# Links between the sublayers of a transformer and a recurrent block, handled four k-tiles at a time

## The chip, the cores and the metric

The kernel runs on one core of one Trainium2 chip, as one launch. The metric is the device time of that core in microseconds (us). A core has a matrix engine (TensorE, "PE" in the profile, its weight loads "PEld"), VectorE ("DVE"), ScalarE ("ACT"), GpSimd ("POOL") and SyncE ("SP"), which issues all DMAs of this kernel.

## The reference, cut to what matters

Two blocks run one after the other in fp32 on 512 tokens of width 1024. The first is two layers of a transformer with 256 further context tokens that share all weights. Each layer has three sublayers, an FFN, a mixing sublayer (two kinds of attention and a Fourier mix), and a second FFN. Between any two of them stands the same arithmetic, per token, with gate, scale and shift vectors per layer, sublayer and stream:

```
y  = rms_norm(sublayer output, g_post)            # end of a sublayer ("post")
x  = x + weight * gate * y
h  = rms_norm(x, g_pre) * (1 + scale) + shift     # start of the next ("pre")
# FFN:  (silu(h @ w1_gate) * (h @ w1_up)) @ w2,   width 2816
```

The second block (a gated recurrence with a state-space scan, then a stick-breaking attention layer) follows on 528 tokens and isn't touched.

## The kernel before, in words

**Layout.** All activations lie transposed: 128 features on the partitions, tokens on the free axis. The 1024 features are eight k-tiles. The residual stream is `X[0..7]`, one tile of 128x528 per k-tile, and `XC` for the context. A sublayer's input is `H[0..7]`, each 128 x 2 x 768, its rounded part "hi" and the remainder "lo"; columns 0 to 511 are latent tokens, 512 to 767 context. Every fp32 product is three matmuls (`mm3`: weight hi by hi, weight hi by lo, weight lo by hi). `Y[0..7]` (128x768 each) gathers a sublayer's output.

**Streams.** The work goes by streams of columns: `cx` (context, 256 wide), `lat` (latent, 512), and its halves `la` and `lb` (256 each). In a sublayer that starts with an FFN, the first of six groups of hidden tiles runs by `cx`, `la`, `lb`; later groups run by halves of all 768 columns with a seven-product scheme (`strassen`) and then `ffn2` over `cx` and `lat`.

**Links.** `link` (line 1240) chains `post` (line 499) and `pre` (line 515) for one stream. Both begin with `rstd`: a column sum of squares on TensorE (L463), a Newton square root on DVE (L474 to L482), a diagonal matrix on DVE (L484), and a matmul with ones (L489) that leaves 1/rms of each token, on all partitions, in PSUM as `r`. Then, for each k-tile, `post` does one DVE instruction for y times gate times r (L507), one DVE add into x (L509), one ACT square (L446, L449) and one add into the running sum (L450, on DVE or POOL by turns). `pre` does, for each k-tile, x times scale times r on DVE (L525), the shift and the rounding on ACT (L526: hi), and the remainder on DVE (L527: lo). So h comes k-tile by k-tile, and the first matmul of the next sublayer can start after the first one.

**Order.** TensorE's order is written by a planner, `run`: generators yield expected times, positive for TensorE time, negative for a wait, and the planner interleaves the one that matters ("crit") with work that fills in. The link of one stream is placed beside another stream's matmuls. The order fixed by these plans is kept on the chip. The other engines' queues and the DMA queue are ordered at build time by the framework's scheduler, and each runs in its order. A flag of the planner, `yfree`, is set by the end of a `post` (L512); in the first mixing sublayer the transposes of the attention values (`vt`, L950) wait for it in the plan, because their results lie in `Y`, and the two rope tables are loaded into `Y` after it.

**PSUM.** `pg` tiles (two buffers) take most products; `bank` tiles (four buffers) are used by `strassen`, by `rstd` in FFN sublayers, and for output tile 1 of `ffn2` (line 771 on). The evacuation of an `ffn2` product is an ACT copy (L786) in the first group and a DVE add into `Y` (L788) in the others.

**Spill.** During an FFN sublayer `X` and `XC` are moved to DRAM and their space holds `strassen`'s sums (`Halves`, line 212 on); they come back in the last group.

Of the kernel before, what the change touches and what calls it, by code (L numbers as in the profile page):

```python
# [211 lines left out]
class Halves:  # L212
# [3 lines left out]
    def __init__(self, b, pool, n):  # L216
        self.b, self.n = b, n
        q = lambda k0, t0: [tuple(b.H[k][:, j, t0 : t0 + n] for j in range(2)) for k in range(k0, k0 + 4)]
        self.B11, self.B12, self.B21, self.B22 = q(0, 0), q(0, n), q(4, 0), q(4, n)
        if n == XW // 2:  # L220
            own = [pool.tile([P, n], F32R, name=f"t{i}") for i in range(11)]
            xc = b.xc.tile([P, KD * NC], F32R, name="tc", tag="xc", bufs=1)
            own += [xc[:, i * n : (i + 1) * n] for i in range(5)]
            own += [b.perm.tile([P, T2], F32R, name=f"tx{k}", tag=f"x{k}", bufs=1)[:, :n] for k in range(KD)]
# [39 lines left out]
class Builder:  # L264
# [228 lines left out]
    def square_x(self, st):  # L493
# [2 lines left out]
            yield -1.8 * (0.2 + 0.9 * st.n / 512)  # L496
        yield -2

    def post(self, st, l, sub, nxt):

        nc = self.nc
        f = st.n / 512
        yield -0.455 * (2.6 + 1.6 * f)
        r = yield from self.rstd(st.s, st.n, D)
        for k in range(KD):
            u = self.ftile(st.n, "u")
            nc.vector.scalar_tensor_tensor(out=u, in0=st.y(k), scalar=self.modG[l][:, st.v, sub, k : k + 1], in1=r, op0=ALU.mult, op1=ALU.mult)  # L507
            x = st.x(k)
            nc.vector.tensor_tensor(out=x, in0=u, in1=x, op=ALU.add)  # L509
            self.add_sq(nxt, k, nxt.x(k), nc.gpsimd if k % 2 == 0 else None)  # L510
            yield -(0.4 + 1.5 * f)
        self.yfree = True  # L512
        yield -1.72 * (2.2 + 1.8 * f)

    def pre(self, st, l, sub):

        nc = self.nc
        r = yield from self.rstd(st.s, st.n, D)
        yield from self.wait_for((l, sub))
        for k in range(KD):  # L520
            u = self.ftile(st.n, "u")
            a = self.modA[l][:, st.v, sub, k : k + 1]
            b = self.modc[l][:, st.v, 24 * sub + k : 24 * sub + k + 1]
            hi, lo = st.h(k)
            nc.vector.scalar_tensor_tensor(out=u, in0=st.x(k), scalar=a, in1=r, op0=ALU.mult, op1=ALU.mult)  # L525
            nc.scalar.activation(hi, u, AF.Identity, bias=b)  # L526
            nc.vector.scalar_tensor_tensor(out=lo, in0=u, scalar=b, in1=hi.bitcast(F32), op0=ALU.add, op1=ALU.subtract)  # L527
            yield -0.85 * (0.1 + 1.2 * st.n / 512)

    def pre2(self, st, gain, d=D):  # L530

# [168 lines left out]
    def strassen(self, pool, l, wi, i0, mids, h):  # L700

        nc = self.nc
        n = h.n
        sub = lambda o, a, b: nc.vector.tensor_tensor(out=o, in0=a, in1=b, op=ALU.subtract)  # L704
        new = lambda nm: pool.tile([P, n], F32, name=nm, tag=nm, bufs=1)
        for ii, mid in enumerate(mids):
            A = self.wsums(self.I["wf1"][l, wi, i0 + ii])
            b1, b4, b2, b3 = (self.bank()[:, :n] for _ in range(4))

            def mm(i, p, b, start):  # L710
                yield from self.mm3(p, A[i], [(k, *x) for k, x in enumerate(b)], start=start, more=not start)
# [17 lines left out]
            sg = pool.tile([P, XW // 2], F32, name="sg", tag="sg", bufs=2)[:, :n]  # L729
# [12 lines left out]
    def ffn1(self, pool, l, wi, i0, mids, ss, ticks=False):  # L742
        nc = self.nc
        for ii, mid in enumerate(mids):
            wg, wu = self.early or self.wblock(self.I["wf1"][l, wi, i0 + ii], 2048, 2)
            self.early = None
            sgs = []
            for w in (wg, wu):
                for st in ss:
                    p = self.pg()[:, : st.n]  # L750
                    yield from self.mm3(p, w, st.rhs())
                    if w is wg:
                        sg = pool.tile([P, XW // 2], F32, name="sg", tag="sg", bufs=2)[:, : st.n]
                        nc.scalar.activation(sg, p, AF.Silu)
                        sgs.append(sg)
                    else:
                        m = self.ftile(st.n, "m")
                        nc.vector.tensor_tensor(out=m, in0=p, in1=sgs.pop(0), op=ALU.mult)  # L758
                        self.split(mid[:, 0, st.cs], mid[:, 1, st.cs], m)
            if ticks and ii % 2 == 0:  # L760
                yield from self.tick()

    def ffn2(self, l, wi, off, mids, ss, first, last, ticks, cb=None):
        nc = self.nc
        n = 2 * len(mids) * P
        for m2 in range(4):
# [3 lines left out]
            for mm in range(2):  # L770
# [6 lines left out]
                for i, st in enumerate(ss):  # L777
# [126 lines left out]
    def mix(self, l, streams, lasts, pend, exits):  # L904
# [4 lines left out]
        with ExitStack() as es:  # L909
# [31 lines left out]
            entry.first = True  # L941

            def vt(kind, i, base, t, offs):

# [240 lines left out]
            side = Task(side())  # L1185
            if full:

                cx.y = lambda k: src[k][:, cx.cs]
            self.run([attention()], [side])
            o_split(lat, (0, 1, 2))  # L1190
            if full:
                self.run(exits[:1], [o_proj(lat)])
                cx.y = lambda k: self.Y[k][:, cx.cs]
# [5 lines left out]
    def block1(self):  # L1199
        self.left, self.right = ExitStack(), ExitStack()  # L1200
        perm = self.perm = self.pool(self.ctx, "perm")
        xtile = lambda k: perm.tile([P, T2], F32, name=f"x{k}", tag=f"x{k}", bufs=1)
        self.X = [xtile(k) for k in range(KD)]
# [10 lines left out]
        AX_, AC_ = [away.tile([P, T2], F32, name=f"ax{k}") for k in range(KD)], away.tile([P, KD * NC], F32, name="ac")  # L1214

        def spill(out, first=False):

            if out and not first:
                self.dma(AC_, self.XC)
                for k in range(KD):  # L1220
                    self.dma(AX_[k], self.X[k])
            if not out:
                xctile()
                self.dma(self.XC, self.I["cin"].rearrange("p k n -> p (k n)") if first else AC_)
                for k in range(KD):
                    self.X[k] = xtile(k)
                    self.dma(self.X[k], self.I["xin"][:, k, :] if first else AX_[k])

        H = self.H = [hy.tile([P, 2, XW], F32R, name=f"h{k}") for k in range(KD)]
        self.Y = [hy.tile([P, XW], F32, name=f"y{k}") for k in range(KD)]  # L1230

        def stream(c0, n, v, xt, x0):
            st = Stream(c0, n, v, xt, x0, lambda k: (H[k][:, 0, c0 : c0 + n], H[k][:, 1, c0 : c0 + n]))
            st.y = lambda k: self.Y[k][:, c0 : c0 + n]
            return st

        lat, cx = stream(XL, NL, 0, self.X, META), stream(XC, NC, 1, XCt, 0)
# [669 lines left out]
```

## Time and profile before

| | |
|---|---|
| runs shown | 3799.95, 3806.11, 3950.75 us; median 3806.11 |
| the profiled execution's own time | 3801.48 us |
| its span (first to last instruction) | 3799.7 us |
| mean granted TensorE clock | 0.959 of full |
| TensorE matmul busy | 92% of the span |
| DVE, ACT, POOL busy | 62%, 45%, 37% |

The span is the time from the first instruction to the last; the execution's own time is 1.8 us longer. Idle time of an engine counts only where TensorE then waits. The granted clock has two levels, 1.0 (2.4 GHz) and 0.5 (1.2 GHz); at the lower one each matmul takes twice as long while it counts as busy.

### The profile page before, as it was taken

The page shows a single profiled execution, that of the slowest core. Times are in us where ns is not written, and L with a number is a line of the kernel's source. Part 1 is how long each engine was busy: PE and PEld are TensorE (multiplying, and loading weights), DVE is VectorE, ACT ScalarE, POOL GpSimd, SP SyncE. Part 2 cuts the span into 40 slices and gives each one's busy share as a digit, 9 for nine tenths or more (in the row PEclk, how much of TensorE's full clock was granted, in tenths as well). Part 3 has the DMA queues.
Part 4 walks back from the last instruction along what each step waited for, and adds up shares of the span by engine and source line. Part 5 has one row for each costly group of instructions (what it writes and reads, how often), then busy time and mean ns, then how long its engine had stood idle before and what let it go on. Part 6 is the DMA issues. An engine that isn't in the chain of part 4 may idle for free.

```text
span 3799.7 us, 61164 instructions
## 1 busy us (share of the span) xinstructions
PE 3504.7 (92%) x23260; PEld 3128.4 (82%) x23260; DVE 2364.0 (62%) x4769; ACT 1708.1 (45%) x3599; POOL 1400.0 (37%) x1151
## 2 busy tenths in 40 slices
PE   7899998998979999988999979888998898999997
PEld 5788897777878888888889967688887877999886
DVE  5844458667784444786445586667567776555546
ACT  5433334456543323454323445554444635635544
POOL 4533343211344333345333431145555433333112
PEclk8999998999989999999999989999999989999998
DMA  7433424212344343443342321242333311234112
GB/s 270 136 125 128 136 75 142 91 56 86 118 127 134 122 134 122 145 145 98 126 138 72 129 91 51 69 133 80 101 99 118 119 44 48 76 116 136 60 48 76
DMA packets 125437, 410.38 MB, mean 108 GB/s; under 512 B 14035, under 2 KB 25814, under 8 KB 123350
## 3 DMA queue, kind: packets, MB, share of 16 engines
q1 hardware_dynamic: 125142, 406.47, 33.5%
q8 instruction: 182, 2.98, 0.3%
q14 instruction: 113, 0.93, 0.1%
HBM read 397.90 MB, written 8.52 MB: 107 GB/s over the span
## 4 chain that ended last, share of the span: by engine, by line
PE 53%; DVE 15%; issue 5%; ACT 5%; POOL 2%; DMA 1%; ACTq 0%; DVEq 0%; POOLq 0%; SPq 0%
PE pg L421 9%; PE pg L422 9%; PE pg L423 9%; PE bank L416 7%; PE bank L421 4%; PE bank L423 3%; PE bank L422 3%; DVE op L353 2%; DVE ss L450 1%; PE po L611 1%; POOL op L353 1%; ACT op L347 1%; PE po L844 1%; PE psw L868 1%; PE po L1830 1%
## 5 line engine op out<-in xcount | busy, mean ns | idle before, releaser
L353 POOL TENSOR_TENSOR op<-raw,op 128x512 fp32r<-128x512 f32 (+1 forms) x660 | 891.2, 1351 | 1488.2 <-ACT op L347 1259.1
L347 ACT CAST op<-raw 128x512 fp32r<-128x512 f32 (+2 forms) x1178 | 709.9, 606 | 821.8 <-PE pg L423 421.3
L353 DVE TENSOR_TENSOR op<-raw,op 128x512 fp32r<-128x512 f32 (+2 forms) x518 | 402.6, 779 | 224.2 <-ACT op L347 217.7
L421 PE MATMUL pg<-h,op 128*128 128x256 f32 (+1 forms) x1440 | 480.1, 333 | 61.7 <-DVE m L758 26.5
L422 PE MATMUL pg<-h,op 128*128 128x256 f32 (+1 forms) x1440 | 467.9, 325 | 4.6 <-DVE h L527 3.3
L423 PE MATMUL pg<-h,op 128*128 128x256 f32 (+1 forms) x1440 | 462.3, 321 | 1.0 <-DVE op L353 0.6
L421 PE MATMUL pg<-mid,op 128*128 128x512 f32 (+1 forms) x1106 | 386.3, 349 | 13.6 <-ACT mid L347 5.3
L422 PE MATMUL pg<-mid,op 128*128 128x512 f32 (+1 forms) x1106 | 379.2, 343 | 1.8 <-DVE mid L353 1.7
L423 PE MATMUL pg<-mid,op 128*128 128x512 f32 (+1 forms) x1106 | 378.8, 342 | 0.0
L421 PEld LDWEIGHTS pg<-h,op 128*128 128x128 f32 x1440 | 293.6, 204 | 86.7 <-DVE m L758 29.2
L422 PEld LDWEIGHTS pg<-h,op 128*128 128x128 f32 x1440 | 292.7, 203 | 23.2 <-DVE h L527 11.1
L423 PEld LDWEIGHTS pg<-h,op 128*128 128x128 f32 x1440 | 293.1, 204 | 16.0 <-DVE op L353 1.0
L416 PE MATMUL bank<-h,op 128*128 128x384 f32 (+1 forms) x1704 | 293.5, 327 | 9.4 <-DVE u L704 9.4
L353 POOL TENSOR_TENSOR op<-ws,op 128x512 fp32r<-128x512 f32 x142 | 191.7, 1350 | 276.8 <-ACT op L347 276.8
L416 PEld LDWEIGHTS bank<-h,op 128*128 128x128 f32 x1704 | 280.9, 190 | 12.3 <-DVE u L704 12.3
L421 PEld LDWEIGHTS pg<-mid,op 128*128 128x128 f32 x1106 | 208.4, 188 | 75.0 <-DVE y L788 29.2
L788 DVE TENSOR_TENSOR y<-pg,y 128x256 f32<-128x256 f32 (+1 forms) x252 | 141.1, 562 | 198.2 <-PE pg L423 197.6
L422 PEld LDWEIGHTS pg<-mid,op 128*128 128x128 f32 x1106 | 208.6, 189 | 27.0 <-DVE mid L353 3.5
L423 PEld LDWEIGHTS pg<-mid,op 128*128 128x128 f32 x1106 | 208.3, 188 | 26.1
L421 PE MATMUL bank<-h,op 128*128 128x384 f32 (+1 forms) x636 | 206.4, 324 | 0.0
L423 PE MATMUL bank<-h,op 128*128 128x384 f32 (+1 forms) x636 | 203.6, 320 | 0.0
L422 PE MATMUL bank<-h,op 128*128 128x384 f32 (+1 forms) x636 | 203.6, 320 | 0.0
(434 smaller groups left out, 8430.1 us busy)
## 6 DMA issues: line engine op xcount, KB each, us to landing
raw<-wf SPq DMA_DIRECT2D x326, 512.0 KB, 3.7
mraw<-wmod SPq DMA_DIRECT2D x128, 512.0 KB, 4.7
raw<-win SPq DMA_DIRECT2D x58, 512.0 KB, 3.7
raw<-ewin SPq DMA_DIRECT2D x48, 512.0 KB, 3.6
raw<-owin SPq DMA_DIRECT2D x40, 512.0 KB, 3.6
raw<-wout SPq DMA_DIRECT2D x32, 512.0 KB, 3.6
raw<-wf SPq DMA_DIRECT2D x32, 384.0 KB, 3.2
raw<-ewout SPq DMA_DIRECT2D x24, 512.0 KB, 3.6
```

The source lines that it names most:

```text
L347: self.nc.scalar.copy(hi, src)
L353: eng.tensor_tensor(out=lo, in0=src, in1=hi.bitcast(F32), op=ALU.subtract)
L416: mm = self.nc.tensor.matmul if not more else lambda *a, **kw: self.nc.tensor.matmul(*a, skip_group_check=True, **kw)
L421: mm(p, lhsT=a, rhs=xh, start=start and i == 0, stop=False)
L422: mm(p, lhsT=a, rhs=xl, start=False, stop=False)
L423: mm(p, lhsT=b, rhs=xh, start=False, stop=stop and i == len(rhs) - 1)
L450: (eng or self.nc.vector).tensor_tensor(out=st.s, in0=st.s, in1=q, op=ALU.add)
L611: nc.tensor.matmul(box["po"][32 * j : 32 * j + 32, :], lhsT=self.cT[:, k, :], rhs=raws[j // 2][:, 512 * (j % 2) : 512 * (j % 2) + 512], st ...
L788: nc.vector.tensor_tensor(out=y, in0=p, in1=y, op=ALU.add)
L844: self.nc.tensor.matmul(o[64 * h : 64 * h + 64, :P], lhsT=cur["v"][h][c], rhs=pTs[h][:, c * P : (c + 1) * P], start=c == 0, stop=c == nt - 1)
L868: nc.tensor.matmul(S[:, h, col : col + ap.shape[1]], lhsT=q[h], rhs=ap, start=True, stop=True)
L1830: nc.tensor.matmul(o[64 * h : 64 * h + 64, :P], lhsT=vt[:m, t, 64 * h : 64 * h + 64], rhs=wTs[h][:m, t, :], start=t == 0, stop=t == j + 1)
```

## The change

`X`, `H` and `Y` become two tiles each that hold four k-tiles side by side, so that one instruction can cover four k-tiles of a stream. For streams whose new x is the next sublayer's input and whose y lies in `Y`, `post` does, for each group of four: one DVE multiply by r (broadcast over the four), four ACT copies that scale by the gate, one DVE add into x, one ACT square, one DVE reduction over the four. Two posts keep the old way (the context after the first mixing sublayer, and the last FFN's). `pre` does, for each four: one DVE multiply by r into `Y` as scratch, four ACT instructions with scale and shift, one ACT copy that rounds (hi), one DVE subtraction (lo). `yfree` is now set at the end of the latent stream's `pre`, and the rope tables are loaded after the whole link. In `ffn2` the odd output tiles go to `bank`, the even ones to `pg`. The spill moves two tiles in place of eight, and `Halves` uses 9 tiles of its own and ten pieces of `X`. `sg` tiles are 512 wide in place of 384; the list of first-group streams (`cx`, `la`, `lb`) is the same in both kernels.

```diff
-            own = [pool.tile([P, n], F32R, name=f"t{i}") for i in range(11)]
+            own = [pool.tile([P, n], F32R, name=f"t{i}") for i in range(9)]
...
+            for g in range(2):
+                x = b.perm.tile([P, 4 * T2], F32R, name=f"tx{g}", tag=f"x{g}", bufs=1)
+                own += [x[:, i * n : (i + 1) * n] for i in range(5)]
...
+    def by4(self, t, n):
+        return t.unsqueeze(1).to_broadcast([P, 4, n])
...
+        if st.y4 is None or nxt is not st:
...
+        else:
+            for g in range(2):
+                y, x = st.y4(g), st.x4(g)
+                nc.vector.tensor_tensor(out=y, in0=y, in1=self.by4(r, st.n), op=ALU.mult)
+                for k in range(4):
+                    nc.scalar.activation(y[:, k, :], y[:, k, :], AF.Copy, scale=gate(4 * g + k))
+                nc.vector.tensor_tensor(out=x, in0=y, in1=x, op=ALU.add)
+                nc.scalar.activation(y, x, AF.Square)
+                s = self.ftile(st.n, "sq") if g else self.stile(st.n)
+                nc.vector.tensor_reduce(out=s, in_=y.rearrange("p k n -> p n k"), axis=AX.X, op=ALU.add)
+                if g:
+                    nc.vector.tensor_tensor(out=st.s, in0=s, in1=st.s, op=ALU.add)
+                else:
+                    st.s = s
+                yield -(1.5 + 7 * f)
...
     def pre(self, st, l, sub):
...
+        for g in range(2):
+            t, (hi, lo) = st.yy4(g), st.h4(g)
+            nc.vector.tensor_tensor(out=t, in0=st.x4(g), in1=self.by4(r, st.n), op=ALU.mult)
+            for k in range(4 * g, 4 * g + 4):
+                nc.scalar.activation(t[:, k % 4, :], t[:, k % 4, :], AF.Identity, scale=self.modA[l][:, st.v, sub, k : k + 1],
+                                     bias=self.modc[l][:, st.v, 24 * sub + k : 24 * sub + k + 1])
+            nc.scalar.copy(hi, t)
+            nc.vector.tensor_tensor(out=lo, in0=t, in1=hi.bitcast(F32), op=ALU.subtract)
+            yield -(1 + 6 * st.n / 512)
+        if st.c0 < NL <= st.c0 + st.n:
+            self.yfree = True
...
-                        p = self.pg()[:, : st.n]
+                        p = (self.bank if m % 2 else self.pg)()[:, : st.n]
...
             def entry():
-                for v in pend:
-                    if self.yfree and entry.first:
-                        entry.first = False
-                        self.dma(cos, I["rope"][:, :NL])
-                        self.dma(sin, I["rope"][:, NL:])
-                    yield v
+                yield from pend
+                self.dma(cos, I["rope"][:, :NL])
+                self.dma(sin, I["rope"][:, NL:])
...
-                for k in range(KD):
-                    self.dma(AX_[k], self.X[k])
+                for g in range(2):
+                    self.dma(AX_[g], self.X4[g])
...
+        self.H4 = [hy.tile([P, 4, 2, XW], F32R, name=f"h{g}") for g in range(2)]
+        self.Y4 = [hy.tile([P, 4, XW], F32, name=f"y{g}") for g in range(2)]
```

## Rows read from the trace of the kernel before

**Rows 1.** The page, busy time by engine: us, share of the span, instructions.

```profile
PE 3504.7 (92%) x23260; PEld 3128.4 (82%) x23260; DVE 2364.0 (62%) x4769; ACT 1708.1 (45%) x3599; POOL 1400.0 (37%) x1151
```

**Rows 2.** Waits of PE: total us, times, longest us.

```profile
PE bank L489 <- DVE dg L484: 37.7, 11, 4.6
...
PE pg L421 <- DVE m L758: 26.5, 13, 7.2
PE pg L421 <- ACT sg L754: 18.0, 6, 5.8
PE bank L463 <- DVE ss L450: 17.4, 7, 6.7
...
PE pg L421 <- DVE y L788: 5.3, 13, 1.0
...
PE pg L421 <- ACT y L786: 2.9, 3, 1.9
```

**Rows 3.** Windows: stretch, length, busy PE, PEld, DVE, ACT, POOL, PEclk, DMA.

```profile
595.00:617.00 22.00, 21.55 (x97) 17.21 (x95) 20.63 (x46) 9.23 (x19) 7.03 (x6) 1.00 0.29 94
617.00:638.00 21.00, 12.42 (x55) 11.39 (x55) 17.90 (x55) 7.84 (x17) 1.99 (x2) 0.59 0.12 39
```

**Rows 4.** Timelines of PE and ACT, entry of the first mixing sublayer: start us, us, instruction, idle before.

```profile
619.88 0.61 PE L463 MATMUL bank<-ones,ss 128*128 128x1 f32 x4 [2.79 <-DVE ss L450]
...
632.23 1.70 PE L463 MATMUL psw<-ones,ss 128*128 128x1 f32 x8
...
635.46 0.38 ACT L972 ACTIVATE aq<-pg 128x256 f32<-128x256 f32 x1 [2.84 <-PE pg L423]
```

**Rows 5.** Timeline of DVE, same stretch.

```profile
626.28 1.27 DVE L525 SCALAR_TENSOR_TENSOR u<-xc,modA,bank 128x256 f32<-128x256 f32 x3 [1.38 <-PE bank L489]
```

**Rows 6.** Timelines of DVE and ACT, entry of the second mixing sublayer.

```profile
2255.59 2.07 DVE L525 SCALAR_TENSOR_TENSOR u<-x,modA,psw 128x512 f32<-128x512 f32 x3 [2.17 <-PE psw L489]
...
2267.43 0.60 ACT L980 ACTIVATE rr<-pg 128x512 f32<-128x512 f32 x1 [1.74 <-PE pg L423]
```

**Rows 7.** Timeline of PE, entry of the first mixing sublayer.

```profile
677.20 1.16 PE L489 MATMUL psw<-dg,ones 128*128 128x128 f32 x8 [0.37 <-DVE dg L484]
679.62 0.38 PE L950 MATMUL pt<-ident,vt 128*128 128x128 f32 x2
```

**Rows 8.** Timelines of DVE and PE, first sublayer's start.

```profile
34.36 1.26 DVE L525 SCALAR_TENSOR_TENSOR u<-xc,modA,psw 128x256 f32<-128x256 f32 x3
...
39.03 0.41 PE L421 MATMUL pg<-h,op 128*128 128x256 f32 x1
...
40.10 0.41 PE L423 MATMUL pg<-h,op 128*128 128x256 f32 x1
...
41.31 0.28 PE L423 MATMUL pg<-h,op 128*128 128x256 f32 x1
```

**Rows 9.** Groups by line and shape, DVE then ACT: busy us, mean ns.

```profile
L450 DVE TENSOR_TENSOR ss<-ss,sq 128x256 f32<-128x256 f32 x136 | 85.5, 629 | 19.5 <-ACT sq L449 10.6 <-POOL ss L450 6.9
L875 DVE TENSOR_REDUCE sm<-psw 128x2 f32<-128x1024 f32 x48 | 58.6, 1220 | 0.8
L527 DVE SCALAR_TENSOR_TENSOR h<-u,modc,h 128x256 fp32r<-128x256 f32 x104 | 56.9, 585 | 3.6 <-ACT h L526 3.5
L509 DVE TENSOR_TENSOR x<-u,x 128x256 f32<-128x256 f32 x64 | 37.6, 587 | 0.6
L525 DVE SCALAR_TENSOR_TENSOR u<-x,modA,bank 128x256 f32<-128x256 f32 x56 | 24.6, 475 | 6.0 <-PE bank L489 6.0
...
L526 ACT ACTIVATE h<-u,modc 128x256 fp32r<-128x256 f32 x104 | 47.2, 501 | 44.8 <-DVE u L525 44.8
L449 ACT ACTIVATE sq<-x 128x256 f32<-128x256 f32 x84 | 34.2, 416 | 40.7 <-DVE x L509 28.4 <-DVE x L1681 5.5 <-DVE x L1845 4.2
L449 ACT ACTIVATE sq<-x 128x512 f32<-128x512 f32 x14 | 8.8, 631 | 14.4 <-DVE x L509 14.3
L1314 ACT ACTIVATE u<-xs,s 128x528 f32<-128x528 f32 x8 | 6.6, 829 | 0.0
```

More of the change, by code (lines that the diff above doesn't have):

```diff
@@ L220, in __init__ @@
         if n == XW // 2:
-            own = [pool.tile([P, n], F32R, name=f"t{i}") for i in range(11)]
+            own = [pool.tile([P, n], F32R, name=f"t{i}") for i in range(9)]
             xc = b.xc.tile([P, KD * NC], F32R, name="tc", tag="xc", bufs=1)
             own += [xc[:, i * n : (i + 1) * n] for i in range(5)]
-            own += [b.perm.tile([P, T2], F32R, name=f"tx{k}", tag=f"x{k}", bufs=1)[:, :n] for k in range(KD)]
+            for g in range(2):
+                x = b.perm.tile([P, 4 * T2], F32R, name=f"tx{g}", tag=f"x{g}", bufs=1)
+                own += [x[:, i * n : (i + 1) * n] for i in range(5)]
             self.T3 = self.B12
@@ L504, in post @@
         r = yield from self.rstd(st.s, st.n, D)
-        for k in range(KD):
[L506 to L512, printed above, removed]
+        gate = lambda k: self.modG[l][:, st.v, sub, k : k + 1]
+        if st.y4 is None or nxt is not st:
+            for k in range(KD):
+                u = self.ftile(st.n, "u")
+                nc.vector.scalar_tensor_tensor(out=u, in0=st.y(k), scalar=gate(k), in1=r, op0=ALU.mult, op1=ALU.mult)
+                x = st.x(k)
+                nc.vector.tensor_tensor(out=x, in0=u, in1=x, op=ALU.add)
+                self.add_sq(nxt, k, nxt.x(k), nc.gpsimd if k % 2 == 0 else None)
+                yield -(0.4 + 1.5 * f)
+        else:
[13 more added lines that the diff above has]
+                yield -(1.5 + 7 * f)
         yield -1.72 * (2.2 + 1.8 * f)
@@ L519, in pre @@
         yield from self.wait_for((l, sub))
[L520 to L528, printed above, removed]
+        for g in range(2):
[9 more added lines that the diff above has]
+            self.yfree = True
     def pre2(self, st, gain, d=D):
@@ L728, in strassen @@
             yield from mm(4, b1, h.B21, False)
-            sg = pool.tile([P, XW // 2], F32, name="sg", tag="sg", bufs=2)[:, :n]
+            sg = pool.tile([P, 512], F32, name="sg", tag="sg", bufs=2)[:, :n]
             nc.scalar.activation(sg, b1, AF.Silu)
@@ L752, in ffn1 @@
                     if w is wg:
-                        sg = pool.tile([P, XW // 2], F32, name="sg", tag="sg", bufs=2)[:, : st.n]
+                        sg = pool.tile([P, 512], F32, name="sg", tag="sg", bufs=2)[:, : st.n]
                         nc.scalar.activation(sg, p, AF.Silu)
@@ L1186, in mix @@
             if full:
[L1188 removed]
+                cx.y, y4, cx.y4 = lambda k: src[k][:, cx.cs], cx.y4, None
             self.run([attention()], [side])
@@ L1192, in mix @@
                 self.run(exits[:1], [o_proj(lat)])
-                cx.y = lambda k: self.Y[k][:, cx.cs]
+                cx.y, cx.y4 = lambda k: self.Y[k][:, cx.cs], y4
             else:
@@ L1201, in block1, with xtiles @@
         perm = self.perm = self.pool(self.ctx, "perm")
-        xtile = lambda k: perm.tile([P, T2], F32, name=f"x{k}", tag=f"x{k}", bufs=1)
-        self.X = [xtile(k) for k in range(KD)]
+        self.X = [None] * KD
+        def xtiles():
+            self.X4 = [perm.tile([P, 4, T2], F32, name=f"x{g}", tag=f"x{g}", bufs=1) for g in range(2)]
+            self.X[:] = [self.X4[k // 4][:, k % 4, :] for k in range(KD)]
+        xtiles()
         xc = self.xc = self.pool(self.right, "xc", "right")
@@ L1213, in block1 @@
         away = self.ctx.enter_context(self.tc.tile_pool(name="away", bufs=1, space=bass.MemoryType.DRAM))
-        AX_, AC_ = [away.tile([P, T2], F32, name=f"ax{k}") for k in range(KD)], away.tile([P, KD * NC], F32, name="ac")
+        AX_, AC_ = [away.tile([P, 4, T2], F32, name=f"ax{g}") for g in range(2)], away.tile([P, KD * NC], F32, name="ac")
         def spill(out, first=False):
@@ L1219, in spill @@
                 self.dma(AC_, self.XC)
-                for k in range(KD):
-                    self.dma(AX_[k], self.X[k])
+                for g in range(2):
+                    self.dma(AX_[g], self.X4[g])
             if not out:
@@ L1224, in spill @@
                 self.dma(self.XC, self.I["cin"].rearrange("p k n -> p (k n)") if first else AC_)
[L1225 to L1230, printed above, removed]
+                xtiles()
+                for g in range(2):
+                    self.dma(self.X4[g], self.I["xin"][:, 4 * g : 4 * g + 4, :] if first else AX_[g])
+        self.H4 = [hy.tile([P, 4, 2, XW], F32R, name=f"h{g}") for g in range(2)]
+        H = self.H = [self.H4[k // 4][:, k % 4] for k in range(KD)]
+        self.Y4 = [hy.tile([P, 4, XW], F32, name=f"y{g}") for g in range(2)]
+        self.Y = [self.Y4[k // 4][:, k % 4, :] for k in range(KD)]
         def stream(c0, n, v, xt, x0):
@@ L1234, in stream @@
             st.y = lambda k: self.Y[k][:, c0 : c0 + n]
+            st.y4 = st.yy4 = lambda g: self.Y4[g][:, :, c0 : c0 + n]
+            st.x4 = lambda g: self.X4[g][:, :, x0 : x0 + n] if xt is self.X else self.XC[:, g * 4 * NC : (g + 1) * 4 * NC].rearrange("p (k n) -> p k n", k=4)
+            st.h4 = lambda g: tuple(self.H4[g][:, :, j, c0 : c0 + n] for j in range(2))
             return st
```

1 line of the change is left out of this document (removed).

## The prediction

> **What bounds the kernel now.** I read the page first, then the waits of PE, then windows and timelines of the entries of sublayers. The page shows PE busy 92% of the span, DVE 62%, ACT 45% [rows 1]: the kernel is bound by the matrix engine, and only what makes PE wait can be won, at most the missing 8%. The waits of PE show where they lie [rows 2]: the two parts of the reciprocal root (37.7 and 17.4 us, behind the DVE of a link) and products that wait for `m`, `sg` and `y`. Windows show the shape of one entry, context into the first mixing sublayer [rows 3]: up to 617 PE is full while DVE works 20.63 of 22 us, then PE does 12.42 of 21 us at a granted clock of 0.59 while DVE works 17.90. The timelines give the chain there: PE waits 2.79 us for the running sum of squares (619.88); from the first k-tile of `pre` (626.28) to the end of the first product (635.46) pass 9.2 us [rows 4, 5]. This link stands open. I counted six more such 256-wide entries in the timeline (1077, 1605, 1686, 2206, 2527, 2563 us), and one at the kernel's start; the other links lie beside another stream's matmuls.
>
> **Base.** The sum is made against the profiled execution, 3801.5 us; the median of the runs is 4.6 us above it.
>
> **Unit prices.** Old: a 256-wide k-tile of `post` costs DVE 0.475 + 0.587 and an add of 0.629 every second tile, ACT 0.416; one of `pre` costs DVE 0.475 + 0.585, ACT 0.501 [rows 9]. New: a DVE pass over 4x256 elements isn't in the trace; the nearest row is a reduction of 1024 elements, 1.22 us, so 1.22 to 1.5 (the upper end by 0.587 against 0.475). An ACT square of 256 takes 0.416, of 512 0.631, so 0.21 per 256 more, and 1024 come to 1.06. An ACT instruction with one per-partition operand is 0.501 against 0.416 without; with two, 0.829 at 528 gives 0.60 at 256; I take 0.59 for `pre` and 0.50 for a gate. Work per link: DVE `post` 11.0 to about 8.5, `pre` 8.5 to about 5.2; ACT 3.3 to 6.1 and 4.0 to 6.8. Over 9 posts and 13 pres that is about 60 us off DVE and 60 us onto ACT. Neither is PE time; the chain counts.
>
> **A, open `pre`, 256 wide, +21.5.** Old, DVE sets the pace and PE follows tile by tile: 9.2 us. New, nothing leaves before a whole four is done: multiply 1.22, four ACT 2.36, copy 1.06, then ACT again 2.36 and 1.06 for the second four (its multiply is hidden), subtract 1.22: 9.3 us; and 11 matmuls of the second four remain. Five matmuls at the lower clock lie between 39.03 and 40.10, 0.214 each [rows 8], so 2.35: 11.65, or +2.45, seven times: 17. At the start of the kernel the old time is 34.36 to 41.6 (the 24th matmul starts at 41.31), 7.2 us [rows 8]; new 11.65: +4.4. Bounds: 8 (ACT at 0.50, and the other stream's sums, 1.70 us at 632.23 [rows 4], fill the gap) to 32 (DVE passes at 1.5, subtraction late).
>
> **B, open 512-wide `pre` at the second mixing sublayer, +5.5.** Old 2255.59 to 2267.43, 11.8 us [rows 6]. New: passes of 2048 elements 2.4, four ACT of 0.80, a copy of 1.9, twice in a row on ACT, and the last subtraction: 2.4 + 5.1 + 5.1 + 2.4 = 15.0, plus 11 matmuls, 2.35: 17.4. Bounds 3 to 7.6.
>
> **C, `yfree` later, +4.** `Y` is now scratch of `pre`, so the transposes of `vt`, which in the plan stood 2.4 us behind the latent stream's root (679.62 after 677.20 [rows 7]), come after a `pre` of some 15 us. Matmuls of the context's projections are in the plan beside it, so most is covered. Bounds 0 to 10. The rope tables are loaded later too; their first user stands behind the first product of the entry [rows 6], which B makes later anyway: costed at nothing, 0 to 3 if a table lands late.
>
> **D, covered links, +2 (0 to 4).** They give their first k-tile later; a planner that knows the new lengths places other matmuls there.
>
> **E, odd tiles of `ffn2` in `bank`, -8.** Products wait for `y` 5.3 and 2.9 us [rows 2]; four buffers more remove at most that. Bounds 0 to -8.2.
>
> **F, `post` ends earlier, -7.** Old 11.0 on DVE, then the last square and add. New, if ACT takes the second four's gates before the first square: 1.2 + 2.0 + 2.0 + 1.5 + 1.06 + 1.2 + 0.6, some 10; in program order some 12. About -1 at seven open links; bounds -14 to +2. The wait at 619.88 [rows 4] shrinks, not to nothing: it then waits for the reduction.
>
> **G, fewer DVE instructions in front of `m` and `sg`, -4.** These waits are 26.5 and 18.0 [rows 2], but most stand under `Halves`, where no link runs. Bounds 0 to -10.
>
> **At nothing:** the spill as 2 transfers in place of 8 on SP's queue, with the same bytes (x is back well before its use; a late piece would show as a wait of L509); `sg` wider; the two `Halves` pieces that move. The diff holds nothing that makes a first group's part by halves: the list of streams is the same in both.
>
> **Sum:** 21.5 + 5.5 + 4 + 2 - 8 - 7 - 4 = +14, so 3815. Bounds together: 3777 to 3860.
>
> **R1, faster, 3776.** In the window ahead of an entry DVE is busy 20.63 of 22 us [rows 3], and its queue holds operand roundings and evacuations of other streams besides the link. If that backlog, not the link's own chain, sets the entry, 3 us less DVE per `post` and `pre` is worth its length: about 2 of the 6 us at each of seven entries and more under F and G (-14, -10, -8 with E, and A at its lower end, +7): -25. Against it: the old `pre` alone has idle slots from ACT (44.8 us ahead of L526 [rows 9]), so the chain runs at its own pace. Here a row and a rule: the two-tensor add L509 takes 587 ns, the scalar-tensor-tensor L525 with r in PSUM 475 [rows 9]. The Trainium skill, "SBUF — State Buffer", section "Who interferes with whom", says that VectorE instructions with two SBUF inputs contend with GpSimd and that those with one, and reductions, don't. By that rule the reduction and the multiply by r (in PSUM) would stay at 1.22 and the adds and subtractions slow down; the trace agrees as far as 587 against 475 goes, and has no reduction from SBUF.
>
> **R2, slower, 3849.** ACT runs in order. About 52 blocks of four put a square or a copy of 1.06 (in place of 0.42 to 0.50) and bursts of four in front of other streams' operand splits and of `sg`. 0.65 us late each, all on the path: +34 on top of +14. It decides from the point where the waits of PE on `sg`, `op` and `mid` of ACT grow by over 30 us together. For: `sg` already costs 18.0. Against: ACT is 45% busy [rows 1]. On this division of labour the Trainium skill, "ScalarE: Activation LUTs", section "Rules for kernel authors", holds that plain multiplies and adds belong on VectorE; no run here shows it yet.
>
> **R3, slower, 3875.** One tile now holds four k-tiles and all streams. If the ordering between instructions is kept by tile and not by columns, a stream's four-tile access waits for another stream's work on the same tile, and six covered links of about 10 us stand open: +60. The trace of before can't show it; the addresses differ, which speaks against.
>
> **How the numbers follow.** Forecast 0.52 (3815, its own range 3790 to 3845), R1 0.28, R2 0.12, R3 0.05, anything else 0.03. The range 3772 to 3850 takes in the forecast, R1's centre, and R2's lower side. About 2% (76 us) is what a measurement tells from no change here: below 3730 lies only an R1 three times its size, 0.03; above 3882 the upper half of R3 and accidents, 0.04; the rest 0.93.
>
> **What would show it.** A: the time from the DVE multiply of `pre` to the first evacuation at the context's entry is 11 to 12 us against 9.2, and ACT, not DVE, is busy through it. B: 17 against 11.8 at the second mixing sublayer. C: `vt` later behind the root. E: the waits on `y` of L786 and L788 gone. F: the last wait of L463 there on a reduction, below 2.79. G: `m` and `sg` down by a few us. DVE's total near 2300 and ACT's near 1770 show the shift. I am wrong if the same chain at 617 to 636 is shorter after than before (then R1), if ACT waits grow throughout (R2), or if whole links lie open where they were covered (R3).

## The result, and the profile after

The changed kernel takes 3830.96 us (median of 4 runs, 3828.80 to 3837.92) against 3803.03 (median of 4). The ratio is 1.0088, with a 95% interval of 1.0073 to 1.0103: slower by some 33 us. One of the four executions of the kernel before (3950.75 us) was in a slower state and is left out of the ratio. The forecast was 3815 us, +14 on its base, with a range of 3772 to 3850: the side and the range hold, the size is about half of what came.

The profiled execution of the changed kernel has a span of 3836.1 us, 36.4 more than before, and a mean granted clock of 0.953 against 0.959. The page's line of busy times by engine (us, share, instructions), to be held against [rows 1]:

```profile
PE 3499.2 (91%) x23260; PEld 3133.8 (82%) x23260; DVE 2333.8 (61%) x4446; ACT 1774.8 (46%) x3651; POOL 1378.9 (36%) x1118
```

PE does the same 23260 matmuls in about the same busy time. Span less busy time grows from 295 to 337 us, so the loss is waiting. The work moved as the forecast had it: ACT +67 us (forecast some +60, to near 1770), DVE only -30 in place of -60.

Where the waiting lies, PE's waits by releaser (us in total, times, longest), to be held against [rows 2]:

```profile
PE bank L491 <- DVE dg L486: 47.3, 12, 7.1
PE pg L423 <- ACT h L547: 45.8, 9, 7.8
PE pg L423 <- DVE m L781: 33.2, 12, 5.7
...
PE pt L968 <- DVE y L972: 13.3, 5, 8.0
...
PE bank L465 <- DVE ss L452: 11.9, 6, 8.7
...
PE pg L425 <- DVE op L355: 6.8, 2, 5.8
...
PE bank L465 <- DVE ss L530: 5.1, 3, 2.2
...
PE pg L423 <- ACT sg L777: 5.0, 4, 1.6
```

Second stands a wait for `h` from ACT, the rounding of the new `pre`: 45.8 us in 9 times, where before the same wait was 12.3 us in 12. The transposes of `vt` wait 13.3 in place of 5.4 us, and the waits of products on `y` are gone. The sums of squares (L465) wait 17.0 us together, as before (17.4).

The entry of the context into the first mixing sublayer, PE, DVE and ACT of the changed kernel (start us, us, instruction, idle before), answers [rows 4, 5]:

```profile
597.30 0.61 PE L491 MATMUL bank<-dg,ones 128*128 128x128 f32 x4
...
615.44 0.58 PE L465 MATMUL bank<-ones,ss 128*128 128x1 f32 x4 [1.51 <-DVE ss L530]
623.10 1.23 PE L491 MATMUL bank<-dg,ones 128*128 128x128 f32 x4 [7.08 <-DVE dg L486]
629.17 0.58 PE L423 MATMUL pg<-h,op 128*128 128x256 f32 x1 [4.85 <-ACT h L547]
```

```profile
617.02 1.47 DVE L452 TENSOR_TENSOR ss<-ss,sq 128x512 f32<-128x512 f32 x2
618.41 0.68 DVE L811 TENSOR_TENSOR y<-bank,y 128x512 f32<-128x512 f32 x1
619.01 0.15 DVE L476 TENSOR_SCALAR v<-bank 128x2 f32<-128x2 f32 x1
...
624.36 2.35 DVE L543 TENSOR_TENSOR y<-xc,bank 128x1024 f32<-128x1024 f32 x2 [1.32 <-PE bank L491]
```

```profile
625.62 2.56 ACT L545 ACTIVATE y<-y,modc,modA 128x256 f32<-128x256 f32 x5 [5.80 <-DVE y L543]
628.09 1.03 ACT L547 CAST h<-y 128x1024 fp32r<-128x1024 f32 x1
...
637.46 0.38 ACT L990 ACTIVATE aq<-pg 128x256 f32<-128x256 f32 x1 [3.62 <-PE pg L425]
```

Rows of the kernel before that stand against these, PE and then DVE:

```profile
600.46 0.61 PE L489 MATMUL bank<-dg,ones 128*128 128x128 f32 x4
...
625.05 1.19 PE L489 MATMUL bank<-dg,ones 128*128 128x128 f32 x4 [4.56 <-DVE dg L484]
627.35 0.58 PE L421 MATMUL pg<-h,op 128*128 128x256 f32 x1 [1.11 <-ACT h L526]
```

```profile
620.52 0.16 DVE L474 TENSOR_SCALAR v<-bank 128x2 f32<-128x2 f32 x1
```

Read it from the top. The sum behind `post` comes 4.4 us earlier than before (615.44 against 619.88), and its last wait is shorter (1.51 against 2.79). Of these 4.4 us, 3.2 were in hand when `post` began: the matmul of its own root stands at 597.30 against 600.46. `post` itself is 1.3 us shorter. Then PE waits 7.08 us for the next root (before: 4.56), since DVE has sums and evacuations of the latent stream in its queue first: the first step of the root (L476) starts 3.6 us after the sum, where before (L474) it started after 0.6. So the root's matmul comes at 623.10 (before: 625.05), and from one root to the next it is 25.8 us against 24.6. From here `pre` loses: ACT runs five modulations and only then a rounding, so the first product starts after a wait of 4.85 us (before: 1.11) and ends 13.1 us after the first DVE instruction (624.36 to 637.46) against 9.2. The wait of 4.84 or 4.85 us stands at all seven open 256-wide entries.

The latent entry of the second mixing sublayer, DVE and ACT of the changed kernel, answers [rows 6]:

```profile
2277.80 4.49 DVE L543 TENSOR_TENSOR y<-x,psw 128x2048 f32<-128x2048 f32 x2 [2.17 <-PE psw L491]
```

```profile
2295.18 0.60 ACT L998 ACTIVATE rr<-pg 128x512 f32<-128x512 f32 x1 [2.13 <-PE pg L425]
```

It takes 17.4 us against 11.8, as worked out. Two waits are new at the first mixing sublayer, both on PE:

```profile
660.89 0.58 PE L425 MATMUL pg<-h,op 128*128 128x256 f32 x1 [5.75 <-DVE op L355]
...
694.57 0.66 PE L968 MATMUL pt<-ident,vt 128*128 128x128 f32 x2 [7.96 <-DVE y L972]
```

The first one is the queue of DVE, in which an operand's remainder stands behind two reductions of the new latent `post`:

```profile
652.77 3.87 DVE L528 TENSOR_REDUCE ss<-y 128x512 f32<-128x2048 f32 x1
656.57 3.67 DVE L528 TENSOR_REDUCE sq<-y 128x512 f32<-128x2048 f32 x1
660.17 0.67 DVE L355 TENSOR_TENSOR op<-raw,op 128x512 fp32r<-128x512 f32 x1
```

The second one is step C, the later `yfree`. The unit costs, DVE and then ACT of the changed kernel (busy us, mean ns), against the prices taken from [rows 9]:

```profile
L548 DVE TENSOR_TENSOR h<-y,h 128x1024 fp32r<-128x1024 f32 x26 | 31.8, 1225 | 41.2 <-ACT h L547 41.2
...
L522 DVE TENSOR_TENSOR y<-y,bank 128x1024 f32<-128x1024 f32 x16 | 19.4, 1214 | 5.2 <-PE bank L491 5.2
...
L528 DVE TENSOR_REDUCE ss<-y 128x256 f32<-128x1024 f32 x9 | 18.5, 2055 | 5.3 <-ACT y L526 5.3
...
L525 DVE TENSOR_TENSOR x<-y,x 128x1024 f32<-128x1024 f32 x12 | 15.4, 1282 | 3.0 <-ACT y L524 3.0
```

```profile
L545 ACT ACTIVATE y<-y,modc,modA 128x256 f32<-128x256 f32 x104 | 54.0, 590 | 37.8 <-DVE y L543 37.4 <-DVE modA L670 0.4
...
L524 ACT ACTIVATE y<-y,modG 128x256 f32<-128x256 f32 x72 | 32.1, 499 | 6.2 <-DVE y L522 6.2
...
L547 ACT CAST h<-y 128x1024 fp32r<-128x1024 f32 x26 | 27.1, 1042 | 0.3
...
L526 ACT ACTIVATE y<-x 128x1024 f32<-128x1024 f32 x12 | 12.7, 1055 | 3.7 <-DVE x L525 3.7
```

All prices but one came out within 2% to 5% of the ones taken (0.59, 0.50, 1.06, 1.22). The one that failed is the reduction, 2.06 us against 1.22: it reads the four k-tiles of one token, which lie far apart in SBUF, and writes 256 elements, where the row it was taken from (L875) reads PSUM and writes 2.

### The profile page after: what moved, and what is told of

Its sections match the earlier page's. It is cut to its first block, busy times and chain, and to the rows that moved or that the text cites. A ratio compares the mean times of both kernels' runs of the same rounds, so it can differ in the third digit from the quotient of the medians.

```text
span 3836.1 us, 60784 instructions
## 1 busy us (share of the span) xinstructions
PE 3499.2 (91%) x23260; PEld 3133.8 (82%) x23260; DVE 2333.8 (61%) x4446; ACT 1774.8 (46%) x3651; POOL 1378.9 (36%) x1118
## 4 chain that ended last, share of the span: by engine, by line
PE 54%; DVE 15%; ACT 6%; issue 5%; POOL 1%; DMA 1%; DVEq 0%; ACTq 0%; POOLq 0%; SPq 0%
PE pg L423 8%; PE pg L424 8%; PE pg L425 8%; PE bank L418 7%; PE bank L423 5%; PE bank L425 5%; PE bank L424 5%; DVE op L355 2%; PE po L634 1%; DVE ss L452 1%; PE po L867 1%; PE po L1858 1%; PE psw L891 1%; ACT op L349 1%; ACT y L545 1%
## 5 line engine op out<-in xcount | busy, mean ns | idle before, releaser
L355 POOL TENSOR_TENSOR op<-raw,op 128x512 fp32r<-128x512 f32 (+1 forms) x660 | 902.6, 1369 | 1561.8 <-ACT op L349 1371.5
L423 PE MATMUL pg<-h,op 128*128 128x256 f32 (+1 forms) x1440 | 479.7, 333 | 84.8 <-ACT h L547 45.8
L355 DVE TENSOR_TENSOR op<-raw,op 128x512 fp32r<-128x512 f32 (+2 forms) x518 | 407.1, 789 | 222.2 <-ACT op L349 215.0
L355 POOL TENSOR_TENSOR op<-ws,op 128x512 fp32r<-128x512 f32 x142 | 191.8, 1351 | 266.7 <-ACT op L349 266.6
L423 PE MATMUL pg<-mid,op 128*128 128x256 f32 (+1 forms) x632 | 221.7, 351 | 3.4 <-ACT mid L349 3.3
L424 PE MATMUL pg<-mid,op 128*128 128x256 f32 (+1 forms) x632 | 217.4, 344 | 1.4 <-DVE mid L355 1.3
L425 PE MATMUL pg<-mid,op 128*128 128x256 f32 (+1 forms) x632 | 216.5, 343 | 0.0
L425 PE MATMUL bank<-mid,op 128*128 128x256 f32 (+1 forms) x632 | 216.2, 342 | 0.0
L423 PE MATMUL bank<-mid,op 128*128 128x256 f32 (+1 forms) x632 | 216.1, 342 | 0.0
L424 PE MATMUL bank<-mid,op 128*128 128x256 f32 (+1 forms) x632 | 216.0, 342 | 0.0
L349 ACT CAST op<-ws 128x512 fp32r<-128x512 f32 x213 | 132.0, 620 | 157.2 <-PE bank L425 93.9
```

Of the source, the lines that this page charges most:

```text
L349: self.nc.scalar.copy(hi, src)
L355: eng.tensor_tensor(out=lo, in0=src, in1=hi.bitcast(F32), op=ALU.subtract)
L423: mm(p, lhsT=a, rhs=xh, start=start and i == 0, stop=False)
L424: mm(p, lhsT=a, rhs=xl, start=False, stop=False)
L425: mm(p, lhsT=b, rhs=xh, start=False, stop=stop and i == len(rhs) - 1)
```

## The experiments

Three theories went in. **H**: the new `pre` costs, by its handover or its order. **P**: the new `post` costs, by its reductions. **E**: the two kinds of banks let evacuations pile up in front of the root. A ratio is to the kernel before, run on the same chip; the median of before was 3798.9, 3798.7 and 3801.3 us in the three groups of four.

**old_pre**: `pre` as before, the rest of the change kept.

```diff
-        for g in range(2):
-            t, (hi, lo) = st.yy4(g), st.h4(g)
...
+        for k in range(KD):
+            nc.vector.scalar_tensor_tensor(out=u, in0=st.x(k), scalar=a, in1=r, op0=ALU.mult, op1=ALU.mult)
+            nc.scalar.activation(hi, u, AF.Identity, bias=b)
+            nc.vector.scalar_tensor_tensor(out=lo, in0=u, scalar=b, in1=hi.bitcast(F32), op0=ALU.add, op1=ALU.subtract)
```

> The changed kernel with `pre` as before (k-tile by k-tile, `yfree` at the end of `post`, rope tables as before); the new `post` and the two kinds of banks stay. Theory H (the new `pre` hands over its first rounded k-tile only after a whole four: the wait before the first product of an open link is 4.85 us against 1.11, seven times, 7.8 against 1.6 at the latent entry, and the vt transposes wait 8.0): this kernel loses all of that, some 26 + 6 + 8 = 40 us against the changed kernel, and stands at 0.996 to 1.000 of the kernel before (3788 to 3803 us). Theory P (the new `post`, with reductions of 2.0 and 3.8 us that hold the queue of DVE, is what costs): 1.005 or more. Theory E (two kinds of banks let the evacuations pile up in front of the Newton steps, wait 7.1 against 4.6 us): 1.004 or more.

3794.3 us, 0.9992 (0.9981 to 1.0003). The whole loss and a little more is in the new `pre`: 0.0096 of 3799 is 36 us. PE's wait for `h` is back where it was:

```profile
PE pg L423 <- ACT h L548: 12.0, 11, 1.6
```

**old_post**: `post` as before, new `pre` and banks kept.

> The changed kernel with `post` as before; the new `pre` and the two kinds of banks stay. H: still 1.006 to 1.012 of the kernel before (3826 to 3849 us), the 4.85 us waits are there. P: 1.000 to 1.003, the 5.75 us wait for an operand of DVE at the entry of the first mixing sublayer is gone.

3826.59 us, 1.0069 (1.0049 to 1.0089): as H has it. The new `post` is worth the difference to 1.0088, about +7 us: small, on the wrong side, and by the two intervals not clear of nothing.

**pg_only**: the two kinds of banks undone.

```diff
-                        p = (self.bank if m % 2 else self.pg)()[:, : st.n]
+                        p = self.pg()[:, : st.n]
```

> The changed kernel with all products of `ffn2` that went to either kind of bank in `pg` again; links new. H: 1.009 to 1.012, since the waits on `y` (5.3 + 2.9 us before) return and the 4.85 us waits stay. E: 1.005 or less, the waits of 7.1 us for the diagonal matrix fall to 4.6.

3844.96 us, 1.0122 (1.0104 to 1.0140). Theory E falls: the banks gain, 0.0034 or 13 us, although the wait for the diagonal matrix does fall without them (longest 5.4 in place of 7.1 us). With the new links and one kind of bank the waits on `y` are more than twice those of [rows 2]:

```profile
PE bank L491 <- DVE dg L486: 39.8, 11, 5.4
...
PE pg L423 <- DVE y L811: 12.2, 15, 2.7
...
PE pg L423 <- ACT y L809: 5.6, 6, 1.8
```

**old_both**: `post` and `pre` as before; banks, tiles of four, spill and `sg` as changed.

> `post` and `pre` as before; of the change there remain the two kinds of banks in `ffn2`, the tiles of four k-tiles, the spill by two transfers and the wider sg. H: 0.996 to 1.000 (3788 to 3803 us): the waits on `y` are gone and no wait of 4.85 us is there. E: 1.003 or more, waits of 7 us for the diagonal matrix in three places.

3789.53 us, 0.9979 (0.9969 to 0.9988): without its links the change is a gain of some 8 us, and there is no 7 us wait for the diagonal matrix (longest 4.5).

**layout_only**: old_both with `ffn2` in `pg` again.

> old_both with the products of `ffn2` in `pg` again: of the change there remain the tiles of four k-tiles, the spill by two transfers and the wider sg. If the two kinds of banks alone make old_both faster: 0.9995 to 1.0005 of the kernel before. If a tile of four k-tiles orders streams against each other (the third rival): above 1.002. If the layout itself gains: below 0.999.

3802.72 us, 1.0013 (1.0001 to 1.0025). The banks are worth 0.0034 here too. The layout with the two-piece spill gains nothing; its interval leaves a cost of 0.4 to 9.5 us, so the 5 us are hardly clear of nothing. A cost of the size of the third rival isn't there.

Then the new `pre` was taken apart. **hand_by_k** keeps the multiply over four and the modulation on ACT, and hands over each k-tile when it is done:

```diff
-            nc.scalar.copy(hi, t)
-            nc.vector.tensor_tensor(out=lo, in0=t, in1=hi.bitcast(F32), op=ALU.subtract)
+                nc.scalar.copy(hi[:, k % 4, :], t[:, k % 4, :])
+                nc.vector.tensor_tensor(out=lo[:, k % 4, :], in0=t[:, k % 4, :], in1=hi[:, k % 4, :].bitcast(F32), op=ALU.subtract)
```

> The changed kernel; in `pre` the multiply by r stays over four k-tiles and the four modulations stay on ACT, but each modulation is followed at once by its own rounding (ACT) and its own subtraction (DVE), so a k-tile is handed over when it is done. Theory H1 (the cost of the new `pre` is the handover by four): the wait before the first product falls from 4.85 to some 2.3 us (1.22 + 0.59 + 0.42 less the 1.1 of before's order), 2.5 us at each of seven entries and more at the latent one: 0.994 to 0.997 of the changed kernel, 1.003 to 1.005 of the kernel before. Theory H2 (it is ACT's work, 0.59 + 0.42 a k-tile in one queue, that sets the pace): no gain on the changed kernel, 1.008 or more, since ACT now has 8 x 0.16 us more of it.

3818.73 us, 1.0048 (1.0032 to 1.0065): 0.0040 of the 0.0096 comes back, as H1 had it. The wait before the first product fell to 2.73 us at this entry, and the entry still takes 11.7 us (624.85 to 636.59; DVE and ACT):

```profile
624.85 2.35 DVE L543 TENSOR_TENSOR y<-xc,bank 128x1024 f32<-128x1024 f32 x2 [1.32 <-PE bank L491]
```

```profile
636.59 0.38 ACT L990 ACTIVATE aq<-pg 128x256 f32<-128x256 f32 x1 [3.49 <-PE pg L425]
```

So the handover by four is part of the cost (some 15 us) and not all of it.

**pre_k_act**: `pre` by single k-tiles, with the modulation and the rounding on ACT as two instructions. The lines stand against those of old_pre:

```diff
-            nc.vector.scalar_tensor_tensor(out=u, in0=st.x(k), scalar=a, in1=r, op0=ALU.mult, op1=ALU.mult)
-            nc.scalar.activation(hi, u, AF.Identity, bias=b)
-            nc.vector.scalar_tensor_tensor(out=lo, in0=u, scalar=b, in1=hi.bitcast(F32), op0=ALU.add, op1=ALU.subtract)
+            nc.vector.tensor_tensor(out=u, in0=st.x(k), in1=r, op=ALU.mult)
+            nc.scalar.activation(u, u, AF.Identity, scale=a, bias=b)
+            nc.scalar.copy(hi, u)
+            nc.vector.tensor_tensor(out=lo, in0=u, in1=hi.bitcast(F32), op=ALU.subtract)
```

> The changed kernel with `pre` by single k-tiles (multiply by r on DVE, modulation in place and rounding on ACT, subtraction on DVE), without scratch in `Y`, with `yfree` and the rope tables as before. It differs from old_pre only in that the modulation is on ACT. H1: as old_pre, 0.998 to 1.002 of the kernel before, the wait before the first product about 1.5 us. H2: halfway to the changed kernel or beyond, 1.004 or more, the first product of an entry paced by ACT at over 1.0 us a k-tile.

3816.52 us, 1.0046 (1.0030 to 1.0063): nothing is handled by four in this `pre`, and 0.0054 (some 20 us) of the cost stays, as H2 had it in size. The entry of the context, ACT and DVE of this kernel:

```profile
628.76 1.09 ACT L548 ACTIVATE u<-u,modc,modA 128x256 f32<-128x256 f32 x2 [5.06 <-DVE u L547]
629.76 0.69 ACT L549 CAST h<-u 128x256 fp32r<-128x256 f32 x2
...
638.86 0.38 ACT L995 ACTIVATE aq<-pg 128x256 f32<-128x256 f32 x1 [3.10 <-PE pg L425]
```

```profile
628.24 1.41 DVE L547 TENSOR_TENSOR u<-xc,bank 128x256 f32<-128x256 f32 x4 [1.32 <-PE bank L491]
...
637.24 0.76 DVE L550 TENSOR_TENSOR h<-u,h 128x256 fp32r<-128x256 f32 x2
```

Two modulations go ahead of two roundings, and the last two subtractions (637.24) stand on DVE behind the first steps of another stream's root: 10.6 us to the first evacuation against 9.2. Measured the same way, the seven entries take 71.1 us in this kernel and 61.8 in old_pre, so they hold some 9 of the 20 us; where the rest lies is open.

**round_dve**: pre_k_act with the rounding on DVE (`nc.vector.tensor_copy(hi, u)`), to tell ACT's load from the length of the chain.

> pre_k_act (1.0046) with the rounding of `pre` on DVE in place of ACT; the modulation stays on ACT. ACT then does 0.59 us a k-tile in place of 1.0, DVE 3 x 0.42 in place of 2 x 0.42. If ACT's queue is what sets the pace of an entry (theory H2): 1.001 or less, near old_pre (0.9992). If the longer chain through four instructions and two engines, or DVE, is what costs (H3): 1.004 or more.

3816.24 us, 1.0047 (1.0028 to 1.0065): no gain, as H3 had it. ACT is busy 34 us less than in pre_k_act (1746.6 against 1780.4) and DVE 23 us more (2372.7 against 2349.7), so work taken from ACT and given to DVE is worth nothing here; that ACT's load by itself costs nothing isn't shown. What this kernel and pre_k_act share, against old_pre, is one more step between the root and the product. On DVE the steps interleave worse: the entry takes 11.5 us (627.11 to 638.61).

**late_free**: step C alone, on post_tree (below): `yfree` at the end of the latent `pre`, rope tables after the whole link.

> post_tree (0.9971) with `yfree` set at the end of the latent stream's `pre` and the rope tables loaded after the whole link, as in the changed kernel, with nothing else of its `pre`. This is the forecast's step C alone. If the step costs what was forecast (+4, 0 to 10 us): 0.998 to 0.9995. If the 8.0 us wait of the transposes is wholly its doing: 0.999 or more. If it is nothing by itself: 0.996 to 0.998.

3790.34 us, 0.9977 (0.9967 to 0.9986), against 0.9971 (0.9958 to 0.9984) of post_tree: +2 us, inside both intervals. The transposes do wait (first line late_free, second post_tree):

```profile
PE pt L969 <- DVE y L973: 12.2, 5, 6.8
```

```profile
PE pt L973 <- DVE y L977: 5.3, 4, 2.2
```

Seven us of waiting came in, and PE's waits grew by some 10 us in all between these two profiled executions (272.0 to 282.3). The ratios differ by 2 us, with some 6 either way, so the price of C isn't told from nothing, nor from the +4 of the forecast.

The last group goes to `post`. **post_tree**: old_pre, with the reduction as two adds.

```diff
-                nc.vector.tensor_reduce(out=s, in_=y.rearrange("p k n -> p n k"), axis=AX.X, op=ALU.add)
+                nc.vector.tensor_tensor(out=y[:, :2, :], in0=y[:, :2, :], in1=y[:, 2:, :], op=ALU.add)
+                nc.vector.tensor_tensor(out=s, in0=y[:, 0, :], in1=y[:, 1, :], op=ALU.add)
```

> old_pre with the strided reduction of the new `post` (2.0 us for 4 x 256, 3.7 to 3.9 for 4 x 512) replaced by two adds (2 x 256, then 256; by rows some 0.7 + 0.45). If the reduction is what the new `post` costs against the old one (old_pre 0.9992 against old_both 0.9979): 0.996 to 0.998. If it is the order on DVE's queue or the coarser steps: as old_pre, 0.999 to 1.000, and the 7.1 us waits for the diagonal matrix stay.

3785.07 us, 0.9971 (0.9958 to 0.9984): 0.0021 or 8 us better than old_pre, so the strided reduction was what made the new `post` a loss. PE's wait for an operand of DVE (L355) fell from 7.5 to 2.9 us, and from one root to the next the context's entry takes 24.7 us in place of 25.8. The 7 us waits at the three context entries stay (longest 7.7); they don't come from the reduction.

The gain isn't in DVE's busy time: it is 2353.6 us, in old_pre 2353.5. Undisturbed, the two adds of a 256-wide stream take 0.68 and 0.41 us, together half of the reduction's 2.06. But 16 of the 44 adds started while GpSimd subtracted an operand's remainder (L355), and each of these ended only 0.3 to 0.55 us after that subtraction, with 1.40 to 1.78 us. None of the other 28 was lengthened. DVE and GpSimd of post_tree (three subtractions follow each other on GpSimd up to 1618.64):

```profile
1614.29 1.52 DVE L529 TENSOR_TENSOR ss<-y 128x256 f32<-128x256 f32 x1
...
1617.42 1.77 DVE L528 TENSOR_TENSOR y<-y 128x512 f32<-128x512 f32 x1
...
1619.72 0.41 DVE L529 TENSOR_TENSOR sq<-y 128x256 f32<-128x256 f32 x1
```

```profile
1613.50 5.14 POOL L355 TENSOR_TENSOR op<-raw,op 128x512 fp32r<-128x512 f32 x3 [6.34 <-ACT op L349]
```

**tree_pg**: post_tree with one kind of bank.

> post_tree with the products of `ffn2` in `pg` again. If new `post` and two kinds of banks add up (banks worth 0.0034 both in old_both against layout_only and in the changed kernel against pg_only): 1.000 to 1.001. If the gain of `post` is only there with the banks: 1.002 or more; if it is larger without them: below 0.999.

3791.35 us, 0.9975 (0.9963 to 0.9988). Third outcome: against layout_only the new `post` by adds gains 0.0038 (14 us), and the banks add almost nothing to it (0.0004). The waits on `y` (8.7 and 2.1 us in tree_pg) are gone in post_tree, but the wait for the diagonal matrix grows from 39.0 to 44.9 us (longest 5.1 and 7.7) and that for the sums of squares from 9.6 to 12.7. So with both, most of the wait moves in front of the root. That both relieve the same place, DVE's backlog at the end of `ffn2`, is the likely reason, and it isn't tested by itself.

**gate_dve**: post_tree with gate and r in one DVE instruction.

```diff
-                nc.vector.tensor_tensor(out=y, in0=y, in1=self.by4(r, st.n), op=ALU.mult)
                 for k in range(4):
-                    nc.scalar.activation(y[:, k, :], y[:, k, :], AF.Copy, scale=gate(4 * g + k))
+                    nc.vector.scalar_tensor_tensor(out=y[:, k, :], in0=y[:, k, :], scalar=gate(4 * g + k), in1=r, op0=ALU.mult, op1=ALU.mult)
```

> post_tree with gate and r in one DVE instruction for each k-tile as before (0.475 x 4 against 1.22 on DVE and 4 x 0.50 on ACT), the rest by four. If the gates on ACT lengthen the chain of `post` (some 1.3 us at each of seven entries): 0.994 to 0.996. If DVE's time is what counts there: 0.998 or more, since DVE has 0.7 us more for each four.

3782.77 us, 0.9955 (0.9942 to 0.9968), the lowest ratio of the study: some 17 us under the kernel before and some 50 under the changed one. It falls where the first expectation had it, but the 0.0016 to post_tree isn't clear of the two intervals. From one root to the next the context's first entry takes 22.9 us against 24.7 in post_tree, so there the gates on ACT had lengthened the chain of `post`; at two later entries (1674 and 2544 us) the same stretch is longer, 27.9 and 27.8 against 25.3 and 24.0. DVE's busy time didn't rise (2350.1 against 2353.6). What the gates cost over the whole kernel is open. What is left of the change in it: add, square and sums by four, two kinds of banks, the layout.

## Why the prediction was right or wrong

**The side and the mechanism were right.** Steps A, B and C said that handing over whole fours behind a modulation on ACT lengthens the open entries, for 21.5 + 5.5 + 4 = 31 us; taking the new `pre` out gives 36 (some 7 either way). B came out at its figure (17.4 us), in part by luck: the last subtraction ends 14.1 us after the start, not 15.0, and the matmuls behind it take 3.2 us, not 2.35. A was low: the seven entries take 11.2 to 13.1 us, where it had 11.65 (before: 8.6 to 9.2, where it had 9.2), and 23 us more together in place of 17. At the context's entry (13.1 us) ACT takes a fifth modulation, one of the second four, ahead of the first rounding, and the other stream's sums (L465) stand between the fours in PE's order as before. At the start of the kernel, for which A had +4.4, the first product ends 3.0 us later (the 100th matmul at 44.6 us against 41.6), but a little later the changed kernel was not behind at all (its 400th matmul ends at 82.6 us, before at 85.0). C's wait is there (7.96 us); its price, +2 us in late_free, isn't told from 0 or from 4.

**F is the term that failed.** "`post` ends earlier, -7" was worth +5 (old_pre against old_both) to +7 us (changed kernel against old_post). Neither is clear of nothing by its intervals, but the first excludes the -7. At the context's entry `post` is indeed 1.3 us shorter, as F had it; then 2.5 us more are lost in front of the root on DVE, whose queue F left out. From one root to the next the seven entries take 5.4 us more together than before. The latent `post` also makes PE wait 5.75 us behind its two reductions. The bounds of F (-14 to +2) were worked out with 1.22 us for a reduction taken from a PSUM row. That a read with the four k-tiles innermost might cost another price wasn't considered. The Trainium skill, "SBUF — State Buffer", section "Door 1: The DMA port swizzle (why `[64,N]` ≈ `[32,N]`)", states that consecutive accesses within one 16-byte line of SBUF go at full bandwidth and that each step to a new line is penalised. By that rule this reduction, whose next element lies 3072 bytes on, pays at every element; the trace agrees in the sign (2.06 us from SBUF, 1.22 from PSUM at the same 1024 elements), but these two rows differ in memory and in what they write as well, so no run here isolates the stride. Post_tree puts the worth of replacing the reduction at 8 us.

**E was too small.** -8, bounded by the two waits on `y`, was 13 us in two comparisons, with intervals that still reach 8, and only 2 us beside the `post` by adds (post_tree against tree_pg). The bound was wrong as a bound: in pg_only the same waits are 17.8 us, since a change elsewhere moves work into them. **G** and **D** can't be told from the rest by these runs: `sg` fell from 18.0 to 5.0 and `m` rose from 26.5 to 33.2.

The sum as measured: layout +5 (hardly clear of nothing), banks -13, `post` +5, `pre` +36, together +33. These are steps from one kernel to the next (layout_only, old_both, old_pre, changed kernel), so they add up by construction. Against the forecast (0 for the layout, -8, -7, and 33 for A to D) F is off by 12, the layout by 5 and E by 5 the other way; G's -4 isn't to be seen by itself. So the size was missed mainly through F, and the lower side of the bounds is a slip of its own: as listed they add up to 3780, not 3777.

**The rivals.** R1 failed: relief of DVE did not pay through the links as built; DVE is busy 21.8 of 22 us ahead of the entry, more than before, as the windows of the changed kernel show (stretch, length, busy PE, PEld, DVE, ACT, POOL, PEclk, DMA):

```profile
595.00:617.00 22.00, 19.51 (x88) 15.64 (x86) 21.79 (x25) 12.91 (x24) 6.17 (x4) 1.00 0.15 51
617.00:638.00 21.00, 9.38 (x40) 8.79 (x41) 11.99 (x35) 8.55 (x16) 1.27 (x1) 0.55 0.18 57
```

Its idea is half right: a `post` by four is a gain once the strided reduction is out of it (0.0038 from layout_only to tree_pg, 0.0024 from old_both to gate_dve). Of the single instructions it had the multiply by r right (1.21 or 1.22 us) and the reduction wrong (2.06 us); adds were lengthened by GpSimd, most of all in post_tree. R2's number (3849) lies about as near as the forecast's, for the wrong reason: the waits on `sg` and `mid` of ACT did not grow (18.0 to 5.0 and 5.3 to 3.3 us) and none on its `op` stands among the waits, and round_dve gained nothing from 34 us less on ACT. The Trainium skill's advice in "ScalarE: Activation LUTs", section "Rules for kernel authors", to keep plain multiplies off ScalarE, agrees with the runs for the modulation (0.0054); for the gates the 0.0016 isn't clear of the intervals. Whether it is the longer chain or ACT's load that costs, these runs don't part. R3 is excluded: layout_only has the shared tiles and post_tree the instructions over four as well, and neither is near +60.

## What to carry to other kernels

Where a matrix engine waits at an entry, count instructions between the last input and the first operand it can use, not the busy time of the engines: fewer, larger instructions lengthen that chain when the consumer could have started on the first piece. Use large instructions where the consumer needs everything anyway (sums before a root), small ones where it needs pieces. Take the price of an instruction from a row with the same access pattern and memory, not only the same number of elements, and look at its longest cases beside what another engine was doing then.

## What the runs showed of the hardware

A DVE reduction over the four k-tiles in SBUF, 1024 elements a partition, took 2.06 us (2.01 for the second four); an element-wise pass over as many took 1.21 to 1.23 in L548. The add of two SBUF tiles (L525) took between 1.21 and 1.96 us, the multiply by r in PSUM (L522, L543) 1.21 or 1.22 every time. In post_tree the adds of 256 elements took 0.41 us, or 1.40 to 1.52 when they started while a GpSimd subtraction ran; the reduction of the changed kernel stayed between 1.94 and 2.08 either way. An ACT instruction with two per-partition operands took 0.59 us at 256 elements, with one 0.50.
